# Sharing the first loads of a grouped instance norm between two transfer queues, by even and odd partitions

## The chip, the cores and the metric

The kernel runs on one core of a Trainium2 chip. The metric is the device time of one execution in microseconds (us), lower is better. All times below are of runs in the fast state with a granted clock of 1.0. A time is a median of several runs; the span of a profile, from its first to its last instruction, is about 1.8 us shorter than the time of the same run.

## The reference

```python
B, G, C_per_g, H, W = 4, 8, 16, 256, 256          # float32
mu = x.mean(axis=(3, 4), keepdims=True)
var = ((x - mu) ** 2).mean(axis=(3, 4), keepdims=True)
out = (x - mu) / np.sqrt(var + 1e-5) * gamma[None, :, :, None, None]
```

There are 512 channels of 65,536 elements, 134.2 MB to read and as much to write.

## The kernel before

A unit is 16 channels, eight partitions to a channel: a tile of 128 partitions by 8192 floats, 4.19 MB (4 MiB). There are 32 units and six buffers. Loads go out on SyncE's queue, but units 1 and 3 on ScalarE's; every store goes out on ScalarE's queue. In the trace each queue finishes its transfers in the order in which they are issued: SyncE's first four loads, issued within 2 us, land one after the other, 19.5 to 76.8 us after their issue. The results are written over the unit in its buffer, so the load of unit u + 6 waits until the store of unit u has landed.

```python
    slots = [data.tile([P, F], F32, name=f"xt{i}") for i in range(AHEAD)]   # AHEAD = 6

    def load(u, queue):
        queue.dma_start(out=slots[u % AHEAD][:], in_=xv[u])

    g_row = singles.tile([1, G * C], F32, name="g_row")
    for u in range(AHEAD):
        if u == 1:
            nc.scalar.dma_start(out=g_row[:], in_=gv[None, :])
        load(u, nc.scalar if u in (1, 3) else nc.sync)
    # ... (constants, gamma spread over the partitions)
    for u in range(U):
        t = slots[u % AHEAD]
        nc.vector.reduce_sum(out=st[:, u, 0:1], in_=t[:], axis=AX.X)
        square = nc.scalar.activation(out=junk[:], in_=t[:], func=ACTF.Square,
                                      accum_out=st[:, u, 1:2])
        # ... (a small matmul sums over the 8 partitions of a channel, then root, reciprocal, scale)
        nc.vector.tensor_scalar(out=t[:], in0=t[:], scalar1=ps[:, 0:1],
                                scalar2=scale[:, u : u + 1], op0=ALU.add, op1=ALU.mult)
        nc.scalar.dma_start(out=ov[u], in_=t[:])
        if u + AHEAD < U:
            load(u + AHEAD, nc.sync)
```

## Time and profile before

| | before |
|---|---|
| time, first three runs | 627.14 us (627.05 to 627.21) |
| profiled span | 625.2 us |
| busy VectorE / ScalarE / TensorE | 71% / 38% / 3% |
| mean transfer rate over the span | 429 GB/s |
| a unit's load, from issue to landing, SyncE's queue (median) | 33.8 us |
| a unit's store, from issue to landing (median) | 67.1 us |

The lines that carry the argument stand in the prediction below. Two more of the kernel before are from the view in order of time (start, length, queue, line of the kernel, operation): when ScalarE's queue issues the gamma row and its two loads, and when SyncE issues load 6, the first one that has to wait for a store.

```profile
0.80 0.53 ACTq L54 DMA_DIRECT2D g_row<-in_gamma_dram  x1
1.37 0.84 ACTq L48 DMA_DIRECT2D xt<-in_x_dram  x2
...
64.50 0.33 SPq L48 DMA_DIRECT2D xt<-in_x_dram  x1
```

The gamma row stands ahead of ScalarE's loads, so its first load is issued 0.57 us later than SyncE's, whose first comes at 0.80.

### The profile page before, as it was taken

The page shows a single profiled execution, that of the slowest core. Times are in us where ns is not written, and L with a number is a line of the kernel's source. Part 1 is how long each engine was busy: PE and PEld are TensorE (multiplying, and loading weights), DVE is VectorE, ACT ScalarE, POOL GpSimd, SP SyncE. Part 2 cuts the span into 40 slices and gives each one's busy share as a digit, 9 for nine tenths or more (in the row PEclk, how much of TensorE's full clock was granted, in tenths as well). Part 3 has the DMA queues.
Part 4 walks back from the last instruction along what each step waited for, and adds up shares of the span by engine and source line. Part 5 has one row for each costly group of instructions (what it writes and reads, how often), then busy time and mean ns, then how long its engine had stood idle before and what let it go on. Part 6 is the DMA issues. An engine that isn't in the chain of part 4 may idle for free.

```text
span 625.2 us, 626 instructions
## 1 busy us (share of the span) xinstructions
PE 21.4 (3%) x80; PEld 19.5 (3%) x80; DVE 443.2 (71%) x162; ACT 238.8 (38%) x98; POOL 1.3 (0%) x9
## 2 busy tenths in 40 slices
PE   2000000000000000000000000000000000000000
PEld 2000000000000000000000000000000000000000
DVE  0699999998867668676687766776667867668620
ACT  0444444444444224443244432344423443224400
POOL 0000000000000000000000000000000000000000
DMA  8999999999999999999999999999999999999998
GB/s 369 436 417 424 434 436 436 436 436 437 434 436 434 426 426 430 434 436 436 436 434 434 436 434 434 430 426 430 434 436 436 436 432 434 436 436 434 426 426 365
DMA packets 9220, 268.46 MB, mean 429 GB/s; under 512 B 1025, under 2 KB 1026, under 8 KB 1026
## 3 DMA queue, kind: packets, MB, share of 16 engines
q10 hardware_dynamic: 4898, 142.61, 52.8%
q1 hardware_dynamic: 4320, 125.83, 46.8%
q14 instruction: 2, 0.02, 0.0%
HBM read 134.22 MB, written 134.22 MB: 429 GB/s over the span
## 4 chain that ended last, share of the span: by engine, by line
another core or an unknown queue 64%; DMA 16%; DVE 13%; SPq 1%; PE 1%; issue 0%; ACT 0%
DMA xt<-in_x_dram 9%; DVE st L103 8%; DMA out_dram<-xt 7%; DVE xt L126 4%; SPq L48 1%; PE ps L112 1%; ACT std L117 0%; DVE nvar L113 0%; DVE rstd L121 0%; DVE scale L123 0%
## 5 line engine op out<-in xcount | busy, mean ns | idle before, releaser
L103 DVE TENSOR_REDUCE st<-xt 128x1 f32<-128x8192 f32 x32 | 277.9, 8684 | 111.2 <-DMA xt<-in_x_dram 111.2
L104 ACT ACTIVATE junk<-xt 128x8192 uint8<-128x8192 f32 x32 | 225.0, 7030 | 272.2 <-DMA xt<-in_x_dram 229.0
L126 DVE TENSOR_SCALAR xt<-xt,ps,scale 128x8192 f32<-128x8192 f32 x32 | 145.6, 4550 | 1.2
L117 ACT ACTIVATE std<-nvar,eps_t 128x1 f32<-128x1 f32 x32 | 9.4, 294 | 79.6 <-DVE nvar L113 79.6
L112 PE MATMUL ps<-st,navg 128*128 128x2 f32 x64 | 17.9, 349 | 568.0 <-DVE st L103 568.0
L112 PEld LDWEIGHTS ps<-st,navg 128*128 128x128 f32 x64 | 16.0, 312 | 569.8 <-issue 569.8
L113 DVE TENSOR_SCALAR nvar<-ps 128x1 f32<-128x1 f32 x32 | 9.2, 287 | 23.8 <-PE ps L112 23.8
L121 DVE RECIPROCAL rstd<-std 128x1 f32<-128x1 f32 x32 | 5.3, 164 | 11.6 <-ACT std L117 11.6
L104 ACT ACTIVATION_READ_ACCUMULATOR junk<-xt 128x1 f32 x32 | 6.0, 186 | 0.0
L123 DVE TENSOR_TENSOR scale<-rstd,g_col 128x1 f32<-128x1 f32 x32 | 5.1, 159 | 1.1
L84 PE MATMUL g_ps<-one,g_rep 1*128 1x1 f32 x16 | 3.5, 346 | 2.9 <-DVE g_rep L79 2.9
L84 PEld LDWEIGHTS g_ps<-one,g_rep 1*128 1x128 f32 x16 | 3.5, 325 | 2.9 <-POOL navg L68 2.9
L90 DVE COPY g_col<-g_ps 128x8 f32<-128x8 f32 x1 | 0.2, 166 | 3.7 <-PE g_ps L84 3.7
L74 ACT ACT_TABLE_LOAD x1 | 1.3, 1283 | 2.2 <-issue 2.2
L79 DVE COPY g_rep<-g_row 1x1024 f32<-1x1024 f32 x1 | 0.7, 681 | 2.1 <-DMA g_row<-in_gamma_dram 2.1
L64 POOL TENSOR_SCALAR_AFFINE_SELECT navg<-navg 128x128 f32<-128x128 f32 x1 | 0.4, 403 | 0.1
L68 POOL TENSOR_SCALAR_AFFINE_SELECT navg<-navg 128x128 f32<-128x128 f32 x1 | 0.4, 398 | 0.1
L63 POOL MEMSET navg<- 128x128 f32 x1 | 0.2, 220 | 0.0
L74 ACT ACTIVATE root_eps<-eps_t 128x1 f32<-128x1 f32 x1 | 0.2, 203 | 0.0
L147 POOL MEMSET const-bfloat16-1.0<- 128x1 bf16 x1 | 0.1, 101 | 0.0
L147 POOL MEMSET const-uint8-127<- 128x1 uint8 x1 | 0.1, 101 | 0.0
L147 POOL MEMSET const-float32-0.0<- 128x1 f32 x1 | 0.1, 98 | 0.3 <-issue 0.3
(3 smaller groups left out, 0.3 us busy)
## 6 DMA issues: line engine op xcount, KB each, us to landing
out_dram<-xt ACTq DMA_DIRECT2D x32, 4096.0 KB, 67.1
xt<-in_x_dram SPq DMA_DIRECT2D x30, 4096.0 KB, 33.8
xt<-in_x_dram ACTq DMA_DIRECT2D x2, 4096.0 KB, 33.3
g_row<-in_gamma_dram ACTq DMA_DIRECT2D x1, 0.5 KB
```

The costliest lines, as they stand in the source:

```text
L48: queue.dma_start(out=slots[u % AHEAD][:], in_=xv[u])
L74: nc.scalar.activation(out=root_eps[:], in_=eps_t[:], func=ACTF.Sqrt)
L79: nc.vector.tensor_copy(out=g_rep[:], in_=g_row[:].rearrange("o (n k) -> o n k", n=NG).unsqueeze(3).to_broadcast([1, NG, K, S]),)
L84: nc.tensor.matmul(out=g_ps[:, n : n + 1], lhsT=g_rep[:, n].rearrange("o k s -> o (k s)"), rhs=one[:], start=True, stop=True,)
L103: nc.vector.reduce_sum(out=st[:, u, 0:1], in_=t[:], axis=AX.X)
L104: square = nc.scalar.activation(out=junk[:], in_=t[:], func=ACTF.Square, accum_out=st[:, u, 1:2],)
L112: nc.tensor.matmul(out=ps[:], lhsT=navg_w, rhs=st[:, u], start=True, stop=True)
L113: nc.vector.tensor_scalar(out=nvar[:, u : u + 1], in0=ps[:, 0:1], scalar1=ps[:, 0:1], scalar2=ps[:, 1:2], op0=ALU.mult, op1=ALU.add,)
L117: nc.scalar.activation(out=std[:, u : u + 1], in_=nvar[:, u : u + 1], func=ACTF.Sqrt, bias=eps_t[:], scale=-1.0,)
L121: nc.vector.reciprocal(out=rstd[:, u : u + 1], in_=std[:, u : u + 1])
L123: nc.vector.tensor_mul(out=scale[:, u : u + 1], in0=rstd[:, u : u + 1], in1=g_col[:, g : g + 1],)
L126: nc.vector.tensor_scalar(out=t[:], in0=t[:], scalar1=ps[:, 0:1], scalar2=scale[:, u : u + 1], op0=ALU.add, op1=ALU.mult,)
```

## The change

Its intent is to start earlier. Before, units 0 and 1 come in side by side: unit 0 lands at 20.3 us, and no unit's compute can start before the first has landed. After, the two queues carry the two halves of unit 0 first, so that it should land in half the time. The halves are the even and the odd partitions.

```diff
-    def load(u, queue):
-        queue.dma_start(out=slots[u % AHEAD][:], in_=xv[u])
+    def load(u, queue, rows=slice(None)):
+        queue.dma_start(out=slots[u % AHEAD][rows], in_=xv[u, rows])
+
+    even, odd = slice(0, P, 2), slice(1, P, 2)
 ...
-    for u in range(AHEAD):
-        if u == 1:
-            nc.scalar.dma_start(out=g_row[:], in_=gv[None, :])
-        load(u, nc.scalar if u in (1, 3) else nc.sync)
+    load(0, nc.sync, even)
+    nc.scalar.dma_start(out=g_row[:], in_=gv[None, :])
+    load(0, nc.scalar, odd)
+    load(2, nc.sync, even)
+    load(1, nc.scalar)
+    load(2, nc.scalar, odd)
+    for u in range(3, AHEAD):
+        load(u, nc.sync)
```

Nothing else differs; the order of instructions on the compute engines is the same.

## The prediction

> **What bounds the kernel now.** I read the whole-page view first, then a table of stretches, then who waits for whom. The page:
>
> ```profile
> span 625.2 us, 626 instructions
> ...
> PE 21.4 (3%) x80; PEld 19.5 (3%) x80; DVE 443.2 (71%) x162; ACT 238.8 (38%) x98; POOL 1.3 (0%) x9
> ...
> DMA  8999999999999999999999999999999999999998
> ...
> HBM read 134.22 MB, written 134.22 MB: 429 GB/s over the span
> ...
> L103 DVE TENSOR_REDUCE st<-xt 128x1 f32<-128x8192 f32 x32 | 277.9, 8684 | 111.2 <-DMA xt<-in_x_dram 111.2
> ...
> out_dram<-xt ACTq DMA_DIRECT2D x32, 4096.0 KB, 67.1
> xt<-in_x_dram SPq DMA_DIRECT2D x30, 4096.0 KB, 33.8
> ```
>
> No compute engine is near full: the busiest, VectorE, has 71%, and its idle time before the big reduction is a wait for loads. The transfer engines show a nine in every slice but the two ends. Each of the 32 units is read once and written once, so 268.4 MB have to move whatever the order. The table of stretches (span, length, five engines, clock, DMA share, GB/s) tells whether the rate is a ceiling:
>
> ```profile
> 0.00:20.00 20.00, 3.54 (x16) 3.48 (x16) 0.85 (x2) 1.49 (x2) 1.29 (x9) 1.00 0.95 393
> 20.00:40.00 20.00, 0.56 (x2) 0.50 (x2) 18.50 (x6) 11.64 (x4) 0.00 (x0) 1.00 0.97 419
> 40.00:60.00 20.00, 1.11 (x4) 1.00 (x4) 17.98 (x7) 10.38 (x6) 0.00 (x0) 1.00 1.00 419
> 60.00:100.00 40.00, 1.12 (x4) 1.01 (x4) 37.31 (x14) 19.57 (x8) 0.00 (x0) 1.00 1.00 433
> 100.00:300.00 200.00, 6.14 (x22) 5.51 (x22) 154.64 (x56) 84.20 (x35) 0.00 (x0) 1.00 1.01 434
> 300.00:500.00 200.00, 6.14 (x22) 5.52 (x22) 143.69 (x55) 74.46 (x31) 0.00 (x0) 1.00 1.00 433
> 500.00:583.00 83.00, 2.23 (x8) 2.00 (x8) 56.53 (x22) 29.80 (x13) 0.00 (x0) 1.00 1.00 433
> ```
>
> From 60 us on the rate is 433 GB/s with a share of 1.00: a ceiling, not an average over gaps. (The two 419s are partly counting: packets of 32 KB are credited whole to one stretch.) Last, the waits of SyncE's queue and the first units in order of time:
>
> ```profile
> SPq L48 <- DMA out_dram<-xt: 536.6, 26, 61.7
> ...
> 20.32 8.69 DVE L103 TENSOR_REDUCE st<-xt 128x1 f32<-128x8192 f32 x1 [13.70 <-DMA xt<-in_x_dram]
> ...
> 35.38 0.35 ACTq L130 DMA_DIRECT2D out_dram<-xt  x1
> 35.78 7.03 ACT L104 ACTIVATE junk<-xt 128x8192 uint8<-128x8192 f32 x1 [5.41 <-DVE xt L126]
> ```
>
> SyncE waits 536.6 us in all for stores, since a load into one of the six buffers must wait until the store out of it has landed. That is the queue working at its ceiling, not a gap: a store takes 67.1 us to land because three others stand before it. The end is full too: the last load lands at 582.87 us; what is then left to store needs the 42 us to 625.2 at full rate. So the kernel is **bound by bytes**: 268.4 MB at 0.433 MB/us is 619.9 us. The profiled span of 625.2 has 5.3 us beyond that, in launch of the first transfer, a slow first 20 us, a hitch near 40 us and the end. The timed runs give 627.14, 1.9 us more than the span.
>
> **What the Trainium skill says.** "DMA: Bandwidth & Descriptors", section "Where 436 GB/s comes from", puts the limit at 435 GB/s over 16 ports of SBUF; the measured 433 agrees. The same page, "Issuing engines are not separate DMA queues", says that transfers of all issuing engines run on the same 16 engines and interleave; the trace agrees: two queues together show 433, and one queue alone in the tail keeps the engines as full. "SBUF — State Buffer", section "Door 1: The DMA port swizzle", says that four neighbouring partitions, and those 32 above, share a port, and that partitions 0 to 63 reach only 8 of 16 ports. Even partitions reach all 16, and so do odd ones; that is the point of splitting by parity. But "The descriptor swizzle" of the DMA page tells which engine serves which partition only for a transfer of 128 partitions, each engine its own port. No load here has 64 rows with a step of two, so no part of this trace shows it.
>
> **The change part by part.**
>
> 1. Unit 0. Before, unit 0 on SyncE's queue and unit 1 on ScalarE's share the engines, so both land together: two units of 4.194 MB at 433 GB/s are 19.4 us, and the first reduction starts at 20.32. After, both queues carry halves of unit 0, 9.7 us, so it should start near 11. Gain of first compute: about 9.5 us. On the path that sets the end: nothing, as the engines move bytes all the same.
> 2. Units 1 to 3. ScalarE's queue holds half of 0, all of 1, half of 2; SyncE's holds half of 0, half of 2, all of 3. At half the rate each, unit 1 lands after 6 MB of its queue and as much of the other, 3 units at 9.7 = 29 us, near 30.5 with the start. Units 2 and 3 land after 4 units, near 40.5. A unit's work on VectorE takes 14.93 us in the first stage (35.26 to 50.19 from reduction to reduction), so unit 0 is done near 26, waits for unit 1 until 30.5, then units 1 to 5 follow each 14.9. Stores 1 and on are issued about 4.5 us earlier, store 0 about 9 us.
> 3. Store 0's place. Before, ScalarE's queue holds units 1 and 3 (8 MB) ahead of store 0; after, half of 0, 1 and half of 2, which is again 8 MB. It starts moving near 40 us either way. Store 1 then has been ready for a long while in both kernels, so the landing of store 0, and with it the issue of load 6 (64 us before), hardly shifts. The gain of parts 1 and 2 ends here, as longer waiting in the queue.
> 4. Added instructions: two more transfers, one on each queue. ScalarE's issues take about 0.4 us each (0.84 for two), at a time when it has no work; two more sets of completion writes are 32 packets of 4 bytes beside 8192 of 32 KB. Cost: 0.1 us at most. Every later instruction has the same order.
>
> Sum: between 0 and -0.5 us if the half loads run at full rate; the median stays at 627.
>
> **The rivals.**
>
> (a) The earlier start pays through to the end. For it: the start is the one stretch below 433 (393 over the first 20 us). Against: launch costs are the same, and nothing between 60 and 583 is idle, so an earlier store only queues longer. Even with no loss anywhere the floor is 619.9 us of span against 625.2, 0.8%. Likely worth 0 to 1 us; over 2% is out of reach.
>
> (b) The half loads run slower. If each of 16 engines gets four successive rows of a half, engine 0 writes partitions 0, 2, 4, 6 and, say, engine 4 writes 32, 34, 36, 38: by the skill's map the same two ports in the same order, so that only 8 of 16 ports work at a time. An estimate from this map and the measured rate: unit 0 takes 19.4 us instead of 9.7, a loss of 9.7; for unit 2 each half packet takes 2.4 us instead of 1.2 while the other queue's packets run normally, again up to 9.7. Together up to 19.4 us, which nothing gives back as the rest is bound by bytes: 646. If engines drift apart, or if the pairing holds only partly, 4 to 10 us, thus 631 to 637. For it: the skill describes a matched layout for 128 partitions only. Against: parity spreads each half over all ports, and an assignment made by the partition would give the same pairing as the full load.
>
> (c) VectorE becomes the bound early. 14.9 us a unit against 19.4 for a unit's two transfers: no. The backlog of loaded units is used up earlier, by about one third of a unit; the wait only moves.
>
> **Range and chances.** I give the full-rate case a good half, with 626 to 628; the slowed case the rest, spread over 629 to 646, of which somewhat under half is over 639.7 (2% above 627.14). Prediction 627.6, a little above the centre of the first case for the weight of the second; 8 times in 10 between 625.6 and 641. Faster by over 2% would need 614.6, below the bytes' floor: 0.01. Slower: 0.17. Within 2%: 0.82.
>
> **What would show it.** In the order of time the first reduction starts near 11 us (20.32 before), the second near 30.5, and store 0 is issued near 26 (35.38 before). SyncE's first wait for a store still ends near 64 us, and stretches after 60 us still show 433. The first 40 us carry the same bytes within 1%. If (b) is right, the first reduction starts near 20 again, the first stretch of 20 us shows far below 393 GB/s, perhaps 220, and the span grows by just the bytes missed. If (a) is right, the first wait ends earlier by what the span loses. A prediction of no change falls if the first 40 us lose more than 5 us of full-rate traffic, or if some later stretch drops below 433.

## The result, and the profile after

The changed kernel takes 627.59 us (627.42 to 627.68, 4 runs); the kernel before, in the same rounds, 627.1 us (626.81 to 627.21, 4 runs). The ratio is 1.0008 with a 95% interval from 0.9991 to 1.0026: the same. (A ratio is the mean time of one kernel's fast runs over that of the other's of the same rounds, so it is not quite the ratio of the medians.)

The page of the changed kernel:

```profile
span 625.9 us, 633 instructions
...
DMA  8999999999999999999999999999999999999998
...
L109 DVE TENSOR_REDUCE st<-xt 128x1 f32<-128x8192 f32 x32 | 277.9, 8685 | 111.5 <-DMA xt<-in_x_dram 111.5
...
out_dram<-xt ACTq DMA_DIRECT2D x32, 4096.0 KB, 67.1
xt<-in_x_dram SPq DMA_DIRECT2D x29, 4096.0 KB, 33.8
```

The wait of the big reduction for loads was 111.2 us and is 111.5; the times to landing are those of before. So VectorE starts earlier and waits as much in all. The table of stretches (span, length, five engines, clock, DMA share, GB/s):

```profile
0.00:20.00 20.00, 3.54 (x16) 3.48 (x16) 4.88 (x3) 5.53 (x3) 1.29 (x9) 1.00 0.89 367
20.00:40.00 20.00, 0.56 (x2) 0.50 (x2) 14.51 (x6) 8.07 (x4) 0.00 (x0) 1.00 1.03 446
40.00:60.00 20.00, 1.11 (x4) 1.00 (x4) 18.03 (x7) 9.86 (x6) 0.00 (x0) 1.00 1.01 419
...
100.00:300.00 200.00, 6.14 (x22) 5.52 (x22) 153.95 (x56) 84.00 (x34) 0.00 (x0) 1.00 1.00 432
```

In the first 40 us, 20 us at 367 and 20 at 446 GB/s are 16.26 MB; before, 393 and 419 made 16.24 MB. The same bytes have moved, only shared out otherwise. Now the first units in order of time:

```profile
15.96 8.69 DVE L109 TENSOR_REDUCE st<-xt 128x1 f32<-128x8192 f32 x1 [9.09 <-DMA xt<-in_x_dram]
...
31.02 0.36 ACTq L136 DMA_DIRECT2D out_dram<-xt  x1
35.30 7.03 ACT L110 ACTIVATE junk<-xt 128x8192 uint8<-128x8192 f32 x1 [9.29 <-DMA xt<-in_x_dram]
...
65.12 0.33 SPq L48 DMA_DIRECT2D xt<-in_x_dram  x1
```

Unit 0's reduction starts at 15.96 us instead of 20.32, and store 0 is issued at 31.02 instead of 35.38, both 4.36 us earlier. But unit 1 now lands only at 35.30 us, while before VectorE began with unit 1 at 35.26. The whole head start is gone with the second unit. Load 6 is issued at 65.12 us, 0.62 later than before. The two profiled spans differ by about as much (0.7 us), but that is no cause: the run with store 0's place, below, issues load 6 at 59.74 us and has a span of 625.7 us.

### The profile page after: what moved, and what is told of

The parts are those of the page before. It is cut to its first block, busy times and chain, and to the rows that moved or that the text cites. A ratio compares the mean times of both kernels' runs of the same rounds, so it can differ in the third digit from the quotient of the medians.

```text
span 625.9 us, 633 instructions
## 1 busy us (share of the span) xinstructions
PE 21.4 (3%) x80; PEld 19.5 (3%) x80; DVE 443.3 (71%) x162; ACT 238.8 (38%) x98; POOL 1.3 (0%) x9
## 2 busy tenths in 40 slices
DMA packets 9252, 268.46 MB, mean 429 GB/s; under 512 B 1057, under 2 KB 1058, under 8 KB 1058
## 4 chain that ended last, share of the span: by engine, by line
another core or an unknown queue 64%; DMA 18%; DVE 10%; SPq 1%; issue 1%; PE 0%; ACT 0%; ACTq 0%
DMA xt<-in_x_dram 11%; DMA out_dram<-xt 8%; DVE st L109 7%; DVE xt L132 3%; SPq L48 1%; PE ps L118 0%; ACT std L123 0%; DVE nvar L119 0%; DVE rstd L127 0%; DVE scale L129 0%; ACTq L48 0%; ACTq L55 0%
## 5 line engine op out<-in xcount | busy, mean ns | idle before, releaser
L109 DVE TENSOR_REDUCE st<-xt 128x1 f32<-128x8192 f32 x32 | 277.9, 8685 | 111.5 <-DMA xt<-in_x_dram 111.5
## 6 DMA issues: line engine op xcount, KB each, us to landing
out_dram<-xt ACTq DMA_DIRECT2D x32, 4096.0 KB, 67.1
```

## The experiments

Twelve kernels were run. "Changed" is always the kernel after the change. Each run was timed beside the kernel before, whose median stayed between 626.9 and 627.1 us.

### Do bytes bound it? One load less

```diff
-        if u + AHEAD < U:
+        if u + AHEAD < U - 1:
```

Unit 31 normalizes what stands in its buffer, so the result is wrong.

> The changed kernel without the last load (unit 31 normalizes what stands in its buffer; a wrong result on purpose), 4.19 MB less of 268.4. If bytes at 433 GB/s bound the kernel throughout, the time falls by 9.7 us to 617.9, within 1. If it were a chain of latencies (store landing, load, compute, store) instead, the removal of a load from the tail would save either nothing or the whole 19.4 us step.

Measured: 617.81 us (617.72 to 618.0), 9.78 less than the changed kernel, where 4.19 MB at 433 GB/s are 9.7. So one load less saves just the time that its bytes take, neither nothing nor a full step of 19.4 us. The kernel is bound by bytes.

### Does the start of compute count? Two and five sums more on unit 0

```diff
-        nc.vector.reduce_sum(out=st[:, u, 0:1], in_=t[:], axis=AX.X)
+        for again in range(3 if u == 0 else 1):      # 6 in the second run
+            nc.vector.reduce_sum(out=st[:, u, 0:1], in_=t[:], axis=AX.X)
```

> The changed kernel with VectorE's sum of unit 0 done three times instead of once, 2 x 8.69 = 17.4 us more before store 0, which is then issued near 48 us instead of 31: later than in the kernel before (35.4). Theory (compute and store 0 have slack until the six loads in flight are all moved, near 60 us): 627.6 within 0.7. Rival (an early store 0 is worth its time): up to 17 us more, or at least the 8 us by which store 0 comes behind the end of the loads on its own queue: 635 to 645.

> The changed kernel with VectorE's sum of unit 0 done six times, 5 x 8.69 = 43.4 us more, so that store 0 is issued near 74.5 us. The six loads in flight are all moved by about 60.5 us, so the transfer engines then stand idle for some 14 us. Theory (only idle time of the transfer engines counts): 627.6 + 14 = 641.6, within 2, and not 627.6 + 43.4 = 671 (compute on the path), nor 627.6 (nothing at the start counts).

Measured: two sums more give 629.51 us (629.08 to 629.8), 1.9 more than the changed kernel. Store 0 is then issued at 48.46 us, 17.4 later, and about one ninth of that shows in the time. So the start is almost free, though not quite as I had said (within 0.7). Most of the 1.9 us lies at the very end: over the last 8 us of the span the transfer engines are busy for a share of 0.48, against 0.64 in the changed kernel, which is 1.3 us. The engines finish further apart; why they do, no run tells. Five sums more give 644.62 us (644.55 to 644.78), 17.0 more, where I had expected 14. The stretch from 60 to 100 us of this run:

```profile
60.00:100.00 40.00, 1.68 (x6) 1.50 (x6) 36.46 (x15) 15.13 (x7) 0.00 (x0) 1.00 0.59 239
```

A share of 0.59 over 40 us leaves 16.4 us without traffic, close to the 17.0 measured. Out of 43.4 us of delay only the part in which the transfer engines had nothing left to do reached the end. I had counted the gap up to store 0's issue, but not the short one after it (a share of 0.48 from 84 to 88 us), in which store 0 has landed and load 6, issued at 85.62 us, has only just begun.

### Does store 0's place count? One unit ahead of it instead of two

```diff
+    load(0, nc.sync)
+    nc.scalar.dma_start(out=g_row[:], in_=gv[None, :])
+    load(1, nc.scalar)
+    for u in range(2, AHEAD):
+        load(u, nc.sync)
```

These lines stand in the place of the changed kernel's opening; no load is halved.

> Whole loads as in the kernel before, but only unit 1 on ScalarE's queue (unit 3 goes to SyncE's), so that store 0 has one unit ahead of it on its queue and not two: the store's place alone. Theory: store 0 begins to move as soon as it is issued, near 35.5 us, and load 6 may be issued some us earlier than 64, but the time stays within 0.7 of 627.1. Rival (store 0's place sets the end): 622 to 625, or as many us more.

Measured: 627.52 us (627.39 to 627.82), ratio to before 1.001 (0.9998 to 1.0022). Load 6 was issued 4.8 us earlier than before, and nothing came of it:

```profile
59.74 0.33 SPq L48 DMA_DIRECT2D xt<-in_x_dram  x1
```

The place of store 0 does not set the end.

### Is the parity of the split needed? Low and high halves

```diff
-    even, odd = slice(0, P, 2), slice(1, P, 2)
+    even, odd = slice(0, P // 2), slice(P // 2, P)
```

> The changed kernel with units 0 and 2 split into partitions 0 to 63 and 64 to 127 in place of even and odd ones. Port theory ([...]a packet of a half takes 2.4 us instead of 1.2): sixteen half packets on each engine, half of them lost time, up to 19.4 us more, 640 to 647 us, and unit 0 lands near 25 us. If two queues with packets for different halves overlap on different engines, less is lost: 632 to 640. Rival (which partitions a half has is of no matter): 627.6 within 0.7 and unit 0 near 16 us.

Measured: 647.55 us (646.84 to 647.61), 19.96 more than the changed kernel, against an estimate of 19.4. Its stretches:

```profile
0.00:20.00 20.00, 3.54 (x16) 3.48 (x16) 0.85 (x2) 1.49 (x2) 1.30 (x9) 1.00 0.98 210
20.00:40.00 20.00, 0.56 (x2) 0.50 (x2) 10.87 (x5) 7.42 (x3) 0.00 (x0) 1.00 0.96 288
...
300.00:500.00 200.00, 6.13 (x22) 5.50 (x22) 143.66 (x55) 75.23 (x33) 0.00 (x0) 1.00 1.00 433
```

The engines are counted as busy (0.98), yet move 210 GB/s: half the ceiling. Once the half loads are over the rate is 433 again. The table of queues says it by the packet (queue, packets, MB, share of 16 engines), from 5 to 25 us, first for this run and then for the changed kernel:

```profile
q10 hardware_dynamic: 64, 2.10, 48.6%
```

```profile
q1 hardware_dynamic: 160, 4.19, 48.6%
```

The first: 48.6% of 16 engines for 20 us are 155.5 us for 64 packets, 2.43 us for a packet of 32 KB. The second: the same 155.5 us for 4.19 MB, that is 128 such packets (the other 32 are completion marks of a few bytes), 1.21 us each. In these runs a row of a low or high half takes twice as long as one of an even or odd half. Unit 0's reduction starts at 27.95 us instead of 15.96.

### What does a half load cost? Unit 0 alone, and all loads in halves

```diff
-    load(2, nc.sync, even)
+    load(2, nc.sync)
     load(1, nc.scalar)
-    load(2, nc.scalar, odd)
```

> The changed kernel with unit 2 whole again on SyncE's queue: only unit 0 is shared, and one transfer less. Theory: the same time within 0.5 of 627.4; unit 1 lands earlier or at the same time as in the changed kernel (35.3 us). If half loads cost 0.25 us each in a transfer count, 627.3; not to be told apart from noise by itself.

Measured: 627.55 us (627.27 to 627.61), ratio 1.0009 (0.9996 to 1.0022). Unit 1's reduction starts at 35.23 us, as in the changed kernel. Its page has the two halves of unit 0 on lines of their own (the last number is us from issue to landing):

```profile
xt<-in_x_dram SPq DMA_DIRECT2D x1, 2048.0 KB, 10.1
xt<-in_x_dram ACTq DMA_DIRECT2D x1, 2048.0 KB, 14.4
```

So SyncE's half came at about 11 us, as predicted for the whole unit, and ScalarE's about 5 us later.

```diff
-            load(u + AHEAD, nc.sync)
+            load(u + AHEAD, nc.sync, even)
+            load(u + AHEAD, nc.sync, odd)
```

> The changed kernel with the other 26 loads (units 6 to 31) issued as even and odd halves too, both on SyncE's queue: the suspected cost of a half load, 26 more transfers instead of 2. If the 0.5 us by which the changed kernel stands above the one before are the price of its two more transfers (0.25 us each), the time is near 627.6 + 6.5 = 634. If they belong to the launch (first packet at 2.1 instead of 1.8 us) or to noise, it stays within 1 us of 627.6.

Measured: 647.97 us (644.47 to 652.65), which is neither answer. The page shows that the regime has changed:

```profile
out_dram<-xt ACTq DMA_DIRECT2D x32, 4096.0 KB, 24.8
xt<-in_x_dram SPq DMA_DIRECT2D x54, 2048.0 KB, 47.2
```

A store lands after 24.8 us instead of 67.1: there is no backlog of stores any more, and the loads are late instead (47.2). The rate was still 433 GB/s from 60 to 100 us and fell to 424 after that. So this run does not price a half load; we come back to it below. The 0.5 us by which the changed kernel stands above the one before is at any rate not the price of its halves, as the run with store 0's place, without any half load, has it as well. All those intervals reach below 1.

### Why did unit 0 not land at 11 us? Gamma moved behind, and onto a third queue

The queues' table of the changed kernel answers most of it. From 0 to 6.7 us, then from 6.7 to 15.2 us:

```profile
q1 hardware_dynamic: 48, 1.57, 65.1%
q10 hardware_dynamic: 2, 0.00, 0.0%
```

```profile
q10 hardware_dynamic: 67, 2.10, 57.1%
q1 hardware_dynamic: 67, 1.67, 45.6%
```

A packet here is one partition's row of 32 KB. Each of the 16 engines moves three rows of SyncE's queue (q1) before the first row of ScalarE's (q10). While ScalarE's 64 rows then come in (2.10 MB), SyncE's queue moves 51 rows (1.67 MB): the last 16 of its half of unit 0, and 35 of unit 2, two on each engine and a little more. Two rows are 2.4 us. The first 48 rows took 1.45 us each instead of 1.21, which is 0.7 us for three. The first row starts at 2.1 us, where the prediction's 11 us left 1.3 for it: 0.8 us. About 1 us remains by subtraction, for the completion of the last rows and the start of the reduction. The runs below ask how much of this the later issue of ScalarE's half explains.

```diff
-    nc.scalar.dma_start(out=g_row[:], in_=gv[None, :])
     load(0, nc.scalar, odd)
+    nc.scalar.dma_start(out=g_row[:], in_=gv[None, :])
```

> The changed kernel with the small gamma transfer moved behind ScalarE's half of unit 0, so that both halves of unit 0 are issued at the same moment. In the changed kernel unit 0 lands at 15.9 us where I had predicted 11. Theory A: ScalarE's half comes late because its queue issued gamma first (1.37 us against 0.80) and SyncE's queue had three packets per engine served before ScalarE's first one; then unit 0 lands here between 11 and 13.5 us. Theory B: the half loads themselves are slow (port conflicts), then it stays near 16. The time for the whole stays at 627.6, within 0.7, under the theory that bytes bound the kernel; if the start of compute were on the path it would fall by 2.5 to 5 us, to 623 to 625.

Measured: unit 0 landed at 14.57 us instead of 15.95, and the time went to 643.65 us (643.04 to 644.88). That is 16.1 us more, with the same bytes and the same split, and 0.57 us difference in one issue. Unit 0's reduction had to wait for gamma until 21.05 us, but a delay of this size is nearly free, as shown above. The second run does without that delay:

```diff
-    nc.scalar.dma_start(out=g_row[:], in_=gv[None, :])
+    nc.gpsimd.dma_start(out=g_row[:], in_=gv[None, :])
```

> The changed kernel with gamma issued from GpSimd, so that both halves of unit 0 are issued at the same moment with nothing ahead of them and nothing small between them on the two queues. Unit 0 lands between 12 and 14.5 us, about 2 us earlier than in the changed kernel. Theory (bytes bound): 627.5 within 0.7 although compute starts earlier still. If gamma's packet from a third queue puts an engine out of step too: 637 to 645.

Measured: unit 0's reduction starts at 14.57 us, the earliest of all runs, and the time is 643.74 us (642.16 to 645.17), the same loss. Its stretches:

```profile
60.00:100.00 40.00, 1.11 (x4) 1.00 (x4) 37.65 (x12) 20.62 (x7) 0.00 (x0) 1.00 1.01 432
100.00:300.00 200.00, 6.13 (x22) 5.50 (x22) 145.86 (x55) 75.83 (x33) 0.00 (x0) 1.00 1.01 424
300.00:500.00 200.00, 5.57 (x20) 5.01 (x20) 138.48 (x50) 74.19 (x30) 0.00 (x0) 1.00 1.00 422
```

The opening is not where the time goes: up to 100 us the rate is 432, and then, with the same transfers as in every other run, it stays near 423 to the end. The table of queues from 100 to 300 us, for this run and then for the changed kernel (q1 carries the loads then, q10 the stores):

```profile
q1 hardware_dynamic: 1466, 42.80, 51.6%
q10 hardware_dynamic: 1451, 42.07, 48.9%
```

```profile
q1 hardware_dynamic: 1487, 43.48, 50.4%
q10 hardware_dynamic: 1488, 42.99, 49.8%
```

Loads: 51.6% of 3,200 engine-us for 42.80 MB (1306 packets of 32 KB) are 1.26 us a packet, against 1.215 in the changed kernel; stores are about as before (1.219 against 1.215). So the load packets themselves take 4% longer on average; it is not a gap. In the single packet records of the trace file, from 100 to 500 us, 84% of the load packets still take the usual 1.21 us and 16% take 1.53 us on average; in the changed kernel 0.1% are longer than 1.23 us. By the rates of the stretches this makes about 12 us; about 6 more come at the end, where the engines no longer finish together (share 0.54 over the last 18.4 us, against 0.86 in the changed kernel). The figures are rounded; the two profiled spans differ by 17.5 us.

That the engines part company can be seen along the way. A big transfer ends with 16 completion marks, one for each engine. In this run the marks of one transfer lie 0.6 us apart from first to last between 60 and 100 us (median), 5.3 between 200 and 300, and 13.3 at the end; the run with gamma behind goes from 2.9 to 12.6. In the changed kernel the distance stays below 1.1 us. A distance of some 3 us does not by itself bring the loss: in the run with two sums more it is 2.6 to 3.3 us from 100 us on, with about 433 GB/s.

### Is it the small transfer? One more on one engine, one more on all, and the old kernel with gamma behind

The gamma row is a single row, which one engine carries: of the 1057 packets under 512 bytes in the changed kernel, the 66 big transfers account for 16 completion marks each, and one is left for gamma. My theory C was that it takes a turn on that engine alone and sets it against the other fifteen.

```diff
     load(0, nc.scalar, odd)
+    g_more = singles.tile([1, G * C], F32, name="g_more")
+    nc.scalar.dma_start(out=g_more[:], in_=gv[None, :])
```

> The changed kernel, gamma first as it is, plus a second 512-byte load of gamma into a tile that nobody reads, in ScalarE's queue right behind its half of unit 0. In the run with gamma behind the half (643.65 us) the packets of the two queues no longer alternate on all 16 engines together, and the rate after 100 us is 424 instead of 433 GB/s. Theory C (a transfer of one row, which one engine alone carries, takes a turn on that engine only and sets it half a turn against the other fifteen; the compute that came late has no part in it): here too about 640 to 645 us and 422 to 426 GB/s after 100 us, with unit 0's reduction near 16 us as in the changed kernel. Theory D (the loss came from the compute that waited for gamma): 627.6 within 0.7.

```diff
     load(0, nc.scalar, odd)
+    g_more = singles.tile([16, (G * C) // 16], F32, name="g_more")
+    nc.scalar.dma_start(out=g_more[:], in_=gv.rearrange("(p f) -> p f", p=16))
```

> As the run with one small transfer more, but the 512 bytes go to 16 partitions of 32 bytes, a row for each of the 16 engines. Theory C: every engine loses the same turn, all stay in step: 627.6 within 1, 433 GB/s after 100 us. Rival (any small transfer in the middle of the bulk does it): 640 to 645 as its neighbour.

```diff
     for u in range(AHEAD):
+        load(u, nc.scalar if u in (1, 3) else nc.sync)
         if u == 1:
             nc.scalar.dma_start(out=g_row[:], in_=gv[None, :])
-        load(u, nc.scalar if u in (1, 3) else nc.sync)
```

> The kernel before, without any half load, with gamma behind unit 1's load on ScalarE's queue instead of ahead of it. Theory C: one engine falls out of step at about 20 us, and the time goes to 637 to 647. Rival (only half loads are sensitive to gamma's place): 627.1 within 1.

Measured: 627.82 us (627.61 to 627.96), 627.45 us (627.41 to 627.75) and 627.04 us (626.95 to 627.24). Nothing is lost in any of the three, and theory C falls. What the two slow runs have in common is that both halves of unit 0 are issued at the same moment, 0.80 us, with nothing ahead of the second. The queues from 4 to 16 us, first for the run with gamma on GpSimd's queue, then for the changed kernel:

```profile
q1 hardware_dynamic: 96, 2.62, 50.6%
q10 hardware_dynamic: 96, 2.62, 50.6%
```

```profile
q1 hardware_dynamic: 112, 3.15, 60.8%
q10 hardware_dynamic: 80, 2.10, 40.5%
```

In the slow run the two queues move the same number of bytes in these 12 us; in the changed kernel SyncE's queue moves 1.05 MB more, two packets on each engine. The slow run with gamma behind shows 96 and 96 packets too; the fast runs with one more small transfer and with unit 0 alone in halves show 112 and 80. It would be easy to say that two queues in balance are the cause. But in the kernel before with gamma behind both queues also start at about 0.80 us, they move 2.62 and 2.56 MB in these 12 us, and nothing is lost. So a balanced start alone does not do it.

Nor is it needed. The run with all loads in halves opens like the changed kernel (112 and 80 packets from 4 to 16 us), and its rate also falls to 424 GB/s after 100 us. Its queues from 100 to 300 us:

```profile
q1 hardware_dynamic: 1605, 42.27, 50.4%
q10 hardware_dynamic: 1476, 42.60, 49.9%
```

That is 1.25 us for a load packet of 32 KB and 1.23 for a store packet, where the changed kernel has 1.215 for both. So three kernels show the slow rate. All three have half loads, but two of them only in the opening and one throughout, while the changed kernel and six other runs with even and odd half loads do not show it. How an opening reaches the length of load packets from 100 us on, whether through which rows are read and written at the same time or otherwise, no run here tells. It stays open.

No version was found that beats the kernel before: with 619.9 us of bytes at 433 GB/s in a span of 625.2 us there is less than 1% to win.

## Why the prediction was right or wrong

The time was right (627.6 said, 627.59 measured), and so was the chain of reasons from bytes to the end. That the two numbers agree to 0.01 us is luck: the prediction's own sum said 627 or a little less, and the 0.6 was added for the weight of a slowed case that did not come. The size of the head start was wrong by half (4.36 us for 9.5), without effect.

- **Bound by bytes: right.** The rate after 60 us is unchanged, one load less is worth 9.78 us, and a delay of 17.4 us at the start shows as 1.9.
- **Part 1, unit 0 "should start near 11": wrong, 15.96.** The term that failed is "both queues carry halves of unit 0, 9.7 us": it supposed that both queues start together and that nothing else moves meanwhile. Neither held. Each engine served three rows of SyncE's queue before the first of ScalarE's, and two rows of unit 2 (2.4 us) before unit 0 was whole; slow first rows cost 0.7 us, a later first row 0.8, and about 1 us passed at the end. With both halves issued at 0.80 us ScalarE's first row still came after two rows of SyncE's on each engine, and unit 0 landed at 14.57: so the later issue accounts for 1.4 of the 5 us, about one row. Why SyncE's queue is served first even then, no run tells.
- **Part 2, unit 1 "near 30.5" and stores "about 4.5 us earlier": wrong, 35.30, and store 1 at 50.36 us against 50.30 before.** It carries on the error of part 1: with SyncE's three rows ahead, unit 1's last row comes later than the prediction's even division puts it. Only store 0 came earlier, by 4.36 us and not 9.
- **Part 3, load 6 "hardly shifts": right.** 65.12 against 64.50 us. The run with store 0's place says more: even 4.8 us earlier did not help.
- **Part 4, added instructions, 0.1 us: not settled.** ScalarE's three issues take 1.78 us together where two took 0.84. The 0.5 us in the medians is inside the interval, and a run without half loads shows it too.
- **Rival (a), an early start pays: wrong, as expected.** The earliest start of all, 14.57 us, belongs to a kernel that takes 643.74 us.
- **Rival (b), slow half loads: not with this split, but with the other.** Even and odd rows take 1.21 us each, as in a full load; low and high halves take 2.43, and cost 19.96 us for an estimate of 19.4. The size of the estimate was right, for a split that the change does not use. Which engine carries which row no run shows, so why parity avoids the loss stays an argument from the map of ports.
- **Rival (c), VectorE as the bound: no.** Its wait for loads did not fall (111.2 to 111.5 us).
- **What the prediction did not see** is that the rate of all that follows can depend on the opening: two kernels with nearly the opening of the changed one ran at about 424 GB/s from 100 us on, and so did the one with all loads in halves. I saw nothing in the profile of the kernel before that pointed to it, and the range allowed for no such loss: these kernels lie above its upper end of 641. That the changed kernel itself escaped it was not foreseen either, so the hit owes something to luck here too.

## What to carry to other kernels

Where the transfer engines have a nine in every slice, first ask whether a change alters the bytes or the rate; here an earlier start only made the queue longer. If a load must be split in two, even and odd partitions are the better split (1.21 us a packet here, against 2.43 for low and high halves), but look at the time of one packet over the whole run to see that it holds: with all loads split so, the kernel took 647.97 us. And when both directions run at the ceiling, time any change in the opening order, however small: here, gamma taken from ahead of one half load, a shift of 0.57 us, went with a rate lower by 2% in the steady state.

## What the Trainium skill lacked or had wrong

- "SBUF — State Buffer", section "Door 1: The DMA port swizzle", says that partitions 0 to 63 reach half the ports. The runs agree: 210 GB/s and 2.43 us for a 32 KB row in low and high halves, against 1.21 us in full loads. It lacks the remedy: 64 rows with a step of two, two such transfers at a time, ran at the full rate in the opening (1.21 us). The page's advice to prefer 32 partitions over 64 (section "The DMA setup-cost knee") is too narrow for such rows; 32 partitions were not run here.
- "DMA: Bandwidth & Descriptors", section "The descriptor swizzle", gives the assignment of rows to engines for 128 partitions only. For 64 rows in steps of two these runs show that no rate is lost; which engine takes which row they do not show.
- "DMA: Bandwidth & Descriptors", section "Issuing engines are not separate DMA queues", says that issuing from several engines only saves the sequencer's time. The runs show a further effect: with unit 0 in halves, the moment at which the second queue's half is issued went with 433 or 424 GB/s in the steady state, 627.6 or 643.7 us. The run with all loads in halves fell to 424 without that. No page has it, and the cause is open.
- No page says how long a head start one queue has over another in a transfer shared by two: SyncE's queue had three rows on each engine ahead, and two when both halves were issued at the same moment. Unit 0 landed at 15.95 and 14.57 us, while its bytes alone need 9.7.
